# Spreading the 144 w_ada pieces differently: ADA1 16 to 24, ADA2 24/26/30 to 18/18/16

## The chip, the core and the metric

One core of one Trainium2 chip runs the whole program. The metric is device time in microseconds, from a median of repeated runs. The engines that appear below: TensorE (PE; PEld is its weight load), VectorE (DVE), ScalarE (ACT), GpSimd (POOL) and the queue of SyncE (SP), from which nearly all transfers are issued.

## What is computed

Two transformer-like networks run one after the other on 256 tokens of width 1024, in f32. Each has two layers, and a layer is feed-forward, token mixer, feed-forward. In the second network every part is modulated by rows that come from a conditioning vector:

```python
def second_block(x, c, w_ada, b_ada, ...):
    cond = jax.nn.silu(c)
    for l in range(DEPTH):
        mod = cond @ w_ada[l] + b_ada[l]
        sh1, sc1, g1, sh2, sc2, g2, sh3, sc3, g3 = jnp.split(mod[:, None, :], N_MOD, axis=-1)
        y = _swiglu(_modulate(x, sh1, sc1), ffn1_w_gate[l], ffn1_w_up[l], ffn1_w_down[l])
        x = _post_norm(x, y, g1, FFN_RES, ln_gain[l, 0], ln_bias[l, 0])
        y = _token_mixer(_modulate(x, sh2, sc2), w_in[l], w_out[l])
        ...
```

`w_ada` has 2 layers x 1024 x 9216 numbers, 75 MB. It depends on nothing that the program computes, so its product with `cond` can be made at any time before the rows are used.

## The kernel before

**Stages.** The program is twelve parts in a row: block 1 is ffn1, mixer, ffn2 for layer 0 and again for layer 1, block 2 the same. In the trace of before block 2 begins near 1160 us; its parts begin near 1160 (ffn1), 1345 (mixer), 1480 (ffn2), 1680 (ffn1 of layer 1), 1890 (mixer) and 2015 us (ffn2).

**A feed-forward part** (`ffn`) reads its weights in 70 units of at most 512 KB: 48 for gate and up, 22 for down. `unit` takes a raw buffer, loads it from SP's queue, and splits it into a high part (a copy on ACT, `wH`) and a low part (a subtraction on DVE, `wL`); in some units the two parts lie in other buffers, which the trace names `X` or `A`. TensorE multiplies three combinations of the parts. Raw buffers come from a ring, in the order of the code: four named `raw`, and two or four more in cells that the trace names `R` and `S`. Block 1 has eight of them, the last part of block 1 and all of block 2 have six.

**A piece of w_ada** (`ada_pieces`) is 128 rows x 1024 columns, 512 KB. It takes the next raw buffer of the same ring, is loaded from the same queue, and DVE adds it, weighted with `cond`, into the accumulator `aacc`: one instruction for each piece, each needing the one before. Eight pieces make one of the 18 modulation rows. Then `ada_row` splits `aacc` (`aaH` on ACT, `aaL` on DVE), sums over the partitions with two matmuls for each half row into a `tr` bank, adds the bias row (`arow`, on DVE), and writes the half row to memory (`mods`) from SP's queue. `mod_row` reads a finished row back, spread over 128 partitions.

**Where pieces are put.** Units 12 to 69 of a feed-forward part each add a fixed rate to a balance, and each whole number of it calls up a piece:

```python
        if self.local and ADA_FROM <= next(self.count) < ADA_TO:
            self.ada_due += self.ada_rate
        while self.ada_due >= 1:
            self.ada_due -= 1
            next(self.ada_gen, None)
```

The rate is `ADA1 / 62` in block 1 and `ADA2[2 * l + j // 2] / 62` in block 2, so 58 of 62 parts of each constant are made. Where a row is needed and not finished, `mod_row` calls up the missing pieces at once, ahead of whatever the code asks for next:

```python
        while self.mods_done < l * 18 + 2 * q + 2:
            next(self.ada_gen, None)
```

This happens in `rows()`, which a feed-forward part calls after its first eight units and a mixer calls after its input projection.

**What sets the order.** The code above only records operations. `Program.emit` gives each a rank by its longest path to the end, places them on engine timelines with estimated durations, four rounds, and writes the instructions out in the order of the planned starts. Each engine then works its own list in order, SP's queue included.

Of the kernel before, what the change touches and what calls it, by code (L numbers as in the profile page):

```python
# [41 lines left out]
MARGIN_G = 1.0  # L42
HALVES = [slice(0, 512), slice(512, 1024)]
ADA_FROM, ADA_TO = 12, 74
ADA1 = 16
ADA2 = [24, 26, 30, 0]

# [631 lines left out]
class Kern:  # L681
# [1286 lines left out]
    def block1(self):  # L1968
        a = self.a
        with ExitStack() as ctx:  # L1970
# [9 lines left out]
            for (what, l), nxt in zip(steps, pres):  # L1980
                r = {}

                def rows():
                    if not self.sp1:
                        self.setup1()
                        self.ada_rate = ADA1 / (ADA_TO - ADA_FROM)
                    r["post"] = self.rowb(a[what + "_post_g"][l])
# [11 lines left out]

                self.ada_rate = ADA1 / (ADA_TO - ADA_FROM) if what != "mix" and self.sp1 else 0.0  # L2000
                if what == "mix":
# [10 lines left out]
    def block2(self):  # L2012
        a = self.a
        with ExitStack() as ctx:
# [5 lines left out]
            for (what, l, j), nxt in zip(steps, steps[1:] + [None]):  # L2020
# [18 lines left out]
                else:  # L2039
                    self.ada_rate = ADA2[2 * l + j // 2] / (ADA_TO - ADA_FROM)  # L2040
                    self.ffn(a[what + "_w_gate_2"][l], a[what + "_w_up_2"][l], a[what + "_w_down_2"][l], rows, tail, NRL - 2)
# [281 lines left out]
```

## Time and profile before

| | |
|---|---|
| median of 3 runs | 2222.63 us (2222.61 to 2223.07) |
| the profiled execution | 2217.46 us |
| its span, first to last instruction | 2215.7 us |
| TensorE busy / weight load busy | 2150.7 us (97%) / 1911.6 us (86%) |
| VectorE / ScalarE busy | 1613.8 us (73%) / 1019.8 us (46%) |
| read from memory | 451.80 MB, 204 GB/s over the span |

The profiled execution is 1.8 us longer than its span and 5.2 us shorter than the median. TensorE is the busy engine; the 65 us in which it does nothing are made of a start of 8 us, an end of 9 us and many short waits between. The windows view gives for a stretch how long each engine was busy, so length minus busy is its idle time there; the granted clock stands behind POOL's column.

### The profile page before, as it was taken

What the parts mean: (1) busy time and instruction counts of PE and PEld (TensorE: products, weight loads), DVE (VectorE), ACT (ScalarE), POOL (GpSimd) and SP (SyncE); (2) the same over time, 40 slices, a digit from 0 to 9 for tenths busy, and PEclk for the clock granted to TensorE, in tenths of its full rate; (3) what the DMA queues carried; (4) which work ended last, traced back from release to release, by engine and by line L of the source; (5) the groups of instructions that cost most, each with busy time, mean ns of one, the idle gap of its engine ahead of it and who ended that gap; (6) DMA issues with size and microseconds to landing.
All of it is one profiled execution on the core that took longest, in us unless ns stands there. A gap on an engine that the chain in (4) does not pass through costs nothing. (4 is left out here: it accounts for less than half of the span.)

```text
span 2215.7 us, 36384 instructions
## 1 busy us (share of the span) xinstructions
PE 2150.7 (97%) x14604; PEld 1911.6 (86%) x14604; DVE 1613.8 (73%) x2301; ACT 1019.8 (46%) x1440; POOL 47.4 (2%) x73
## 2 busy tenths in 40 slices
PE   8999999999999999999999999999998999999998
PEld 7998988898899798879979988778986987777996
DVE  6666897767666689866667678687878768868554
ACT  6444644545445455454435444534444434544441
POOL 0000001000000000100000000000000000000000
PEclk9999999999999999999999999999999999999999
DMA  9674414767677542466767675468886767537661
GB/s 358 209 246 153 144 57 145 257 213 268 195 242 234 171 135 78 154 220 220 256 212 253 226 266 185 138 206 271 274 281 222 266 224 252 183 126 243 182 194 63
DMA packets 208313, 455.30 MB, mean 205 GB/s; under 512 B 20808, under 2 KB 56008, under 8 KB 208144
## 3 DMA queue, kind: packets, MB, share of 16 engines
q1 hardware_dynamic: 207856, 451.87, 62.5%
q8 instruction: 114, 1.87, 0.3%
q10 hardware_dynamic: 288, 1.11, 0.1%
q14 instruction: 55, 0.45, 0.1%
HBM read 451.80 MB, written 1.12 MB: 204 GB/s over the span
## 5 line engine op out<-in xcount | busy, mean ns | idle before, releaser
L639 DVE TENSOR_TENSOR wL<-raw,wH 128x1024 fp32r<-128x1024 f32 (+1 forms) x375 | 437.8, 1177 | 170.8 <-ACT wH L639 169.2
L639 ACT CAST wH<-raw 128x1024 fp32r<-128x1024 f32 (+1 forms) x375 | 377.4, 1013 | 393.9 <-PE pa L639 118.6
L639 PE MATMUL pa<-hT,wH 128*128 128x256 f32 x3008 | 547.1, 283 | 3.0 <-ACT wH L639 3.0
L639 PEld LDWEIGHTS pa<-hT,wH 128*128 128x128 f32 x3008 | 469.4, 192 | 5.6 <-ACT wH L639 3.4
L639 PE MATMUL pa<-hT,wL 128*128 128x256 f32 x1504 | 425.5, 283 | 0.0
L639 PE MATMUL pa<-hT,X 128*128 128x256 f32 x2400 | 307.9, 283 | 4.0 <-ACT X L639 3.9
L639 PEld LDWEIGHTS pa<-hT,X 128*128 128x128 f32 x2400 | 297.3, 189 | 6.5 <-ACT X L639 4.4
L639 PEld LDWEIGHTS pa<-hT,wL 128*128 128x128 f32 x1504 | 289.1, 192 | 0.2 <-DVE wL L639 0.2
L639 PE MATMUL pj<-wH,hT 128*128 128x256 f32 (+1 forms) x768 | 202.9, 341 | 1.3 <-DVE G L639 0.7
L639 DVE TENSOR_TENSOR X<-raw,X 128x1024 fp32r<-128x1024 f32 (+1 forms) x103 | 117.3, 1139 | 58.9 <-ACT X L639 55.9
L639 DVE TENSOR_TENSOR wL<-R,wH 128x1024 fp32r<-128x1024 f32 (+1 forms) x101 | 119.6, 1185 | 54.9 <-ACT wH L639 54.5
L639 PEld LDWEIGHTS pj<-wH,hT 128*128 128x128 f32 x768 | 132.3, 189 | 24.6 <-issue 5.8
L639 ACT CAST wH<-R 128x1024 fp32r<-128x1024 f32 (+1 forms) x101 | 102.8, 1018 | 105.5 <-PE pa L639 48.8
L639 ACT CAST X<-raw 128x1024 fp32r<-128x1024 f32 (+1 forms) x103 | 101.0, 981 | 79.6 <-PE pa L639 37.7
L639 PE MATMUL pa<-wH,hT 128*128 128x512 f32 x384 | 131.2, 402 | 2.6 <-DVE hT L639 1.1
L639 PE MATMUL pj<-wL,hT 128*128 128x256 f32 (+1 forms) x384 | 126.0, 329 | 3.2 <-DVE wL L639 3.2
L639 PE MATMUL pj<-hT,wH 128*128 128x256 f32 (+1 forms) x672 | 126.8, 288 | 0.1
L639 PEld LDWEIGHTS pj<-hT,wH 128*128 128x128 f32 (+1 forms) x672 | 102.3, 186 | 3.3 <-issue 0.7
L639 DVE SCALAR_TENSOR_TENSOR aacc<-raw,cols,aacc 128x1024 f32<-128x1024 f32 x74 | 94.7, 1280 | 13.8 <-DMA raw<-in_w_ada_dram 13.2
L639 PE MATMUL pb<-wH,A 128*128 128x512 f32 x288 | 102.5, 396 | 0.0
L639 PE MATMUL pa<-wH,A 128*128 128x512 f32 x288 | 102.2, 395 | 0.0
L639 PE MATMUL pj<-hT,wL 128*128 128x256 f32 (+1 forms) x336 | 95.0, 283 | 0.0
(420 smaller groups left out, 3429.6 us busy)
## 6 DMA issues: line engine op xcount, KB each, us to landing
raw<-in_ffn_w_gate_dram SPq DMA_DIRECT2D x110, 512.0 KB
raw<-in_ffn_w_down_dram SPq DMA_DIRECT2D x109, 512.0 KB
raw<-in_w_in_dram SPq DMA_DIRECT2D x108, 512.0 KB
raw<-in_ffn_w_up_dram SPq DMA_DIRECT2D x89, 512.0 KB
raw<-in_w_ada_dram SPq DMA_DIRECT2D x85, 512.0 KB
R<-in_ffn_w_up_dram SPq DMA_DIRECT2D x53, 512.0 KB
R<-in_ffn_w_down_dram SPq DMA_DIRECT2D x53, 512.0 KB
R<-in_w_ada_dram SPq DMA_DIRECT2D x48, 512.0 KB
```

Source lines behind the costliest of these rows:

```text
L639: getattr(self.prog.tc.nc, self.eng).__getattribute__(name)(*[real(x) for x in a], **{q: real(x) for q, x in k.items()})
```

## The change

Two constants change, the sum of the pieces does not.

```diff
-ADA1 = 16
-ADA2 = [24, 26, 30, 0]
+ADA1 = 24
+ADA2 = [18, 18, 16, 0]
```

Counted on SP's list, the parts from the first to the last feed-forward part load these numbers of pieces: before 14, 15, 15, 15 in block 1 and 23, 34, 28, 0 in block 2; now 22, 22, 23, 22 and 17, 17, 15, 4, with 2 more at the end of the last mixer. In the 34 of before there are about 10 that `mod_row` called up at the start of the part, since the rows of layer 1 were due there; now 106 pieces are made by then and 92 are wanted. The last two rows are due at the end of the last mixer and in the last feed-forward part: before, all 144 pieces were made by then, now 138 are, and 6 are called up there.

VectorE at the start of ffn2 of layer 0 in block 2. `hT` is the transposed input of the part for the second half of the tokens, `G` and `A` belong to the part's first products, `x_223` is the second half of the residual. Before:

```order
L639 TENSOR_TENSOR hT_266<-tr,hT_259 128x4x128
L639 SCALAR_TENSOR_TENSOR aacc<-raw,cols,aacc 128x1024 x2
L639 SCALAR_TENSOR_TENSOR aacc<-R,cols,aacc 128x1024 x2
L639 SCALAR_TENSOR_TENSOR aacc<-raw,cols,aacc 128x1024 x2
L639 SCALAR_TENSOR_TENSOR x_223<-x_223,mv,S 128x512 x2
L639 TENSOR_TENSOR G<-G,pa 128x512
L639 TENSOR_TENSOR A<-tr,A 128x4x128
L639 TENSOR_TENSOR aaL<-aacc,aaH 128x512
L639 TENSOR_TENSOR arow<-arow,tr 1x512
L639 TENSOR_TENSOR X<-raw,X 128x1024
```

Now, in the same place:

```order
L639 TENSOR_TENSOR hT_266<-tr,hT_259 128x4x128
L639 SCALAR_TENSOR_TENSOR x_223<-x_223,mv,S 128x512
L639 TENSOR_TENSOR wL<-raw,wH 128x1024
L639 TENSOR_TENSOR wL<-R,wH 128x1024
L639 TENSOR_TENSOR X<-raw,X 128x1024
L639 TENSOR_TENSOR wL<-raw,wH 128x1024 x2
L639 TENSOR_TENSOR X<-R,X 128x1024
L639 TENSOR_TENSOR G<-G,pa 128x512
```

Six pieces in a row and the first half row are gone from there, and the splits of the next units stand directly behind `hT`.

VectorE at the start of ffn2 of layer 1, the last feed-forward part. Before:

```order
L639 TENSOR_TENSOR hT_266<-tr,hT_259 128x4x128
L639 SCALAR_TENSOR_TENSOR x_223<-x_223,mv,L 128x512
L639 TENSOR_TENSOR wL<-raw,wH 128x1024
L639 TENSOR_TENSOR wL<-R,wH 128x1024
L639 TENSOR_TENSOR X<-raw,X 128x1024
L639 TENSOR_TENSOR wL<-raw,wH 128x1024 x2
```

Now:

```order
L639 TENSOR_TENSOR hT_266<-tr,hT_259 128x4x128
L639 SCALAR_TENSOR_TENSOR aacc<-raw,cols,aacc 128x1024 x2
L639 SCALAR_TENSOR_TENSOR aacc<-R,cols,aacc 128x1024 x2
L639 SCALAR_TENSOR_TENSOR x_223<-x_223,mv,L 128x512
L639 TENSOR_TENSOR aaL<-aacc,aaH 128x512
L639 TENSOR_TENSOR X<-raw,X 128x1024
L639 TENSOR_TENSOR wL<-raw,wH 128x1024 x2
```

Four pieces in a row and the first half of the last row came to this place.

SP's queue at the end of the last mixer. Before:

```order
L639 DMA S<-mods 128x1024
L639 DMA raw<-in_w_out_dram 128x1024
L639 DMA R<-in_ffn_w_up_dram 128x2x512
L639 DMA raw<-in_w_out_dram 128x1024
L639 DMA raw<-in_ffn_w_gate_dram 128x2x512
```

Now:

```order
L639 DMA S<-mods 128x1024
L639 DMA raw<-in_w_ada_dram 128x1024
L639 DMA R<-in_ffn_w_up_dram 128x2x512
L639 DMA raw<-in_w_ada_dram 128x1024
L639 DMA raw<-in_w_out_dram 128x1024
L639 DMA mods<-arow 1x512
L639 DMA R<-in_ffn_w_up_dram 128x2x512
L639 DMA S<-mods 128x1024
L639 DMA raw<-in_w_out_dram 128x1024
```

The last unit of `w_out` now stands behind two pieces, behind the write of a half row and behind the read of that row. On VectorE's list two pieces, two instructions on the half row and two 128x1024 products with the late row stand there in front of the mixer's tail; none of them stood there before.

## Rows read from the trace of the kernel before

**Rows 1.** The page: busy time of the engines, share of the span, instructions.

```profile
PE 2150.7 (97%) x14604; PEld 1911.6 (86%) x14604; DVE 1613.8 (73%) x2301; ACT 1019.8 (46%) x1440; POOL 47.4 (2%) x73
```

**Rows 2.** Windows: stretch, length, busy time by engine, granted clock, DMA share, GB/s.

```profile
640.00:720.00 80.00, 80.00 (x629) 77.55 (x628) 53.94 (x59) 39.11 (x49) 0.00 (x0) 1.00 0.72 232
1200.00:1320.00 120.00, 120.00 (x852) 112.13 (x851) 86.14 (x93) 54.05 (x66) 0.00 (x0) 1.00 0.74 242
1352.00:1362.00 10.00, 7.58 (x47) 6.14 (x47) 9.49 (x18) 1.86 (x4) 0.92 (x1) 1.00 0.54 166
1488.00:1516.00 28.00, 22.92 (x127) 18.89 (x126) 24.08 (x26) 8.33 (x11) 0.00 (x0) 0.96 0.80 261
1510.00:1520.00 10.00, 7.70 (x49) 7.50 (x50) 5.50 (x6) 6.01 (x7) 0.00 (x0) 0.83 0.89 297
1520.00:1640.00 120.00, 120.00 (x891) 113.98 (x890) 95.01 (x103) 55.11 (x69) 0.00 (x0) 1.00 0.82 274
1655.00:1670.00 15.00, 13.41 (x57) 10.16 (x56) 10.80 (x12) 5.04 (x5) 0.00 (x0) 1.00 0.59 186
1675.00:1700.00 25.00, 20.07 (x89) 14.77 (x90) 22.95 (x31) 9.45 (x12) 0.92 (x1) 1.00 0.79 259
1812.00:1822.00 10.00, 6.50 (x34) 5.68 (x34) 5.60 (x7) 4.50 (x6) 0.00 (x0) 0.83 0.54 198
1885.00:1903.00 18.00, 13.59 (x73) 9.91 (x72) 17.25 (x27) 4.22 (x6) 0.99 (x1) 1.00 0.81 245
1990.00:2012.00 22.00, 21.52 (x99) 16.61 (x98) 19.03 (x31) 9.05 (x13) 0.93 (x1) 1.00 0.57 194
2020.00:2030.00 10.00, 6.86 (x33) 4.97 (x32) 9.31 (x15) 1.17 (x2) 0.93 (x1) 1.00 0.82 263
2030.00:2058.00 28.00, 28.00 (x194) 25.87 (x193) 24.23 (x27) 16.09 (x18) 0.00 (x0) 1.00 0.80 249
```

**Rows 3.** Groups by shape, VectorE: one piece, and the addition of one half row.

```profile
L639 DVE SCALAR_TENSOR_TENSOR aacc<-raw,cols,aacc 128x1024 f32<-128x1024 f32 x74 | 94.7, 1280 | 13.8 <-DMA raw<-in_w_ada_dram 13.2
L639 DVE TENSOR_TENSOR arow<-arow,tr 1x512 f32<-1x512 f32 x36 | 24.1, 670 | 12.0 <-PE tr L639 11.6 <-DMA arow<-in_b_ada_dram 0.4
L639 DVE TENSOR_SCALAR arow<-arow 1x512 f32<-1x512 f32 x24 | 9.8, 410 | 0.2
```

**Rows 4.** Timeline of the start of ffn2, layer 0: VectorE, SP's queue, TensorE.

```profile
1488.53 2.59 DVE L639 SCALAR_TENSOR_TENSOR aacc<-raw,cols,aacc 128x1024 f32<-128x1024 f32 x2
...
1495.12 1.70 SPq L639 DMA_DIRECT2D raw<-in_ffn_w_gate_dram  x2
...
1512.26 1.21 PE L639 MATMUL pa<-hT,wH 128*128 128x256 f32 x8 [3.03 <-ACT wH L639]
```

**Rows 5.** Timeline of the end of that part: VectorE, SP's queue, ScalarE.

```profile
1657.60 1.28 DVE L639 SCALAR_TENSOR_TENSOR aacc<-R,cols,aacc 128x1024 f32<-128x1024 f32 x1
...
1658.90 0.34 SPq L639 DMA_DIRECT2D R<-in_ffn_w_down_dram  x1
...
1663.38 1.04 ACT L639 CAST A<-R 128x1024 fp32r<-128x1024 f32 x1 [5.63 <-DMA R<-in_ffn_w_down_dram]
```

**Rows 6.** TensorE's timeline and SP's waits (us, times, longest), 1812 to 1822.

```profile
1817.30 3.02 PE L639 MATMUL pa<-hT,X 128*128 128x256 f32 x11 [3.40 <-ACT X L639]
...
SPq L639 <- DVE X L639: 6.0, 1, 6.0
```

**Rows 7.** Timeline of VectorE in two turns between parts of block 2.

```profile
1675.79 1.28 DVE L639 SCALAR_TENSOR_TENSOR aacc<-raw,cols,aacc 128x1024 f32<-128x1024 f32 x1
...
1886.63 0.67 DVE L639 TENSOR_TENSOR arow<-arow,tr 1x512 f32<-1x512 f32 x1
```

**Rows 8.** Timeline of the last mixer's end: SP's queue, ScalarE, TensorE.

```profile
1992.56 0.33 SPq L639 DMA_DIRECT2D raw<-in_w_out_dram  x1
...
1998.22 1.05 ACT L639 CAST wH<-raw 128x1024 fp32r<-128x1024 f32 x1 [1.76 <-DMA raw<-in_w_out_dram]
...
2011.67 1.04 PE L639 MATMUL tr<-con,h 128*128 128x128 f32 x8
```

## Prediction

> **What bounds the kernel now.** The page comes first: TensorE is busy for 97% of the span [rows 1], so nothing that is added beside it costs time unless TensorE comes to wait. The next view is therefore the windows, read for what TensorE lacks in each stretch. Inside the feed-forward parts it lacks nothing: 80.00 of 80 us in a part of block 1 that carries 15 pieces, 120.00 of 120 in ffn1 of block 2 with 23, and 120.00 of 120 even in the gate and up products of the part with 34 [rows 2]. What is lacking lies at certain places of block 2, and the third view, the timelines, says what is done there. At the start of ffn2 of layer 0, VectorE works six pieces one after the other; the raw buffers are in their hands, the next gate loads leave SP's queue only at 1495.12, and TensorE ends up waiting 3.03 us for a weight [rows 4]. So the price of a piece is not its 1.28 us on VectorE [rows 3] but the time at which it gives its raw buffer back, and whose load stands behind it.
>
> **What the move takes away in block 2.** Five places, each by length minus TensorE's busy time, compared with a like place that has no pieces in its way [rows 2].
> - Start of ffn2, layer 0: 28 - 22.92 = 5.1 us idle between 1488 and 1516. The same stretch of the last feed-forward part, which has no pieces, has 28.00 of 28. Behind it the granted clock is 0.83 over the ten microseconds from 1510, which is a time at the lower level of 1.2 GHz instead of 2.4 and costs 1.7 us more. Together 6.8. In the new order the row of VectorE there is the one that the last part had before, so I take all of it as saved.
> - End of that part: 15 - 13.41 = 1.6. A piece held `R` until 1658.9, and the load of a down unit that waited for it came 4.5 us later [rows 5].
> - Turn from there to ffn1 of layer 1: 25 - 20.07 = 4.9, against 10 - 6.86 = 3.1 in the turn to the last part: 1.8 above the like. Pieces stand between the tail and the transposed input [rows 7]; in the new order none does.
> - Last gate and up units of ffn1, layer 1, near 1814: 10 - 6.50 = 3.5, and the clock 0.83 again for 1.7: 5.2. SP stood 6.0 us behind one buffer there [rows 6].
> - Turn from there to the last mixer: 18 - 13.59 = 4.4 against 10 - 7.58 = 2.4 in the other mixer of block 2: 2.0. A half row's additions stand among the splits and the transposes there [rows 7]; in the new order they are gone.
>
> That is 6.8 + 1.6 + 1.8 + 5.2 + 2.0 = 17.4 us in all. The first, third and fifth hang on instructions whose place I can see emptied: 10.6, taken in full. The second and fourth, 6.8, hang on which buffer of the ring stood behind which, and with 17 pieces instead of 34 and 15 instead of 28 the ring still turns. ffn1 of layer 0 with 23 pieces had neither, so the bounds are 0 and 6.8, and I take half, 3.4. Saved: 14.0 us.
>
> **What the move adds in block 1.** Seven or eight pieces more in each of four parts: 8 x 1.28 = 10.2 us of VectorE and 4.2 MB a part. VectorE was busy 53.94 of 80 us there and has some 26 us free in each 80; the transfers were at 0.72 of their time [rows 2]. The nearest row is the part with 23 pieces, which has the new number, only six raw buffers where block 1 mostly has eight, and no idle time inside. I take nothing; the upper bound is the stall near 1814 once in each of the four parts, 4 x 5.2 = 20.8. If a part does not hide them, each piece that TensorE waits for costs up to 1.28 us. The turns between the parts of block 1 keep one piece here and lose one there; I take nothing for them either.
>
> **What it adds at the end of block 2.** Six pieces are called up late, where before none was.
> - End of the last mixer. VectorE's list gets two pieces (2.56), the half row (0.67 + 0.41) [rows 3] and two products with the late row (128x1024 as a piece is, so by its row 2.56) in front of the tail: 6.2 us. In the 22 us there VectorE was idle for 22 - 19.03 = 3.0 [rows 2]. What doesn't fit is 3.2. The transfers give the same size: the last `w_out` load was issued at 1992.56 and reached ScalarE at 1998.22 [rows 8]; now it stands behind the write of a half row and the read of that row, about four microseconds later. TensorE was not waiting before its transposes at 2011.67 [rows 8], so most of a delay shows. I take 3.0, with bounds of 0 and 6.2.
> - Start of the last part. Four pieces in a row instead of six, and no second batch behind them as ffn2 of layer 0 had; the next gate loads stand ahead of the pieces on SP's queue or just behind. Bounds 0 and 6.8 (the whole loss of that other start). I take 0.5, near the lower end, because the first eight units are in hand and give TensorE some 10 us of products (48 for half the tokens, at 6.86 us for 33 in the turn [rows 2]) over four pieces' 5.1.
>
> One rule of the skill speaks against this. In the trace the clock fell behind the single waits of 3.03 and 3.40 us [rows 4, 6], and stayed at 1.00 through 4.9 us of idle time in several short waits between 1675 and 1700 [rows 2]. The Trainium skill (TensorE: Matmul & The Clock Gate, section "A second HAM failure mode: psum-queue depth-cycling") says that frequent very short idle times between groups of matmuls can make the clock swing too. By that rule the short waits at the new place would cost another 1.7 us, and the forecast would be 2213.8; by the row they cost no clock. I go by the row.
>
> **The sum.** -14.0 + 3.0 + 0.5 = -10.5 us. On the profiled execution, 2217.46, that gives 2207.0. The median of the runs lies 5.2 us above that execution, and I take the difference as it is: 2222.63 - 10.5 = 2212.1, told as 2212.
>
> **The rivals.**
> - *The waits belong to the order, not to the number of pieces.* The planner writes the whole program in another order, and a ring whose buffers change hands with any piece can stall at new places. For: the stall near 1814 came in a part with fewer pieces than its neighbour, which had none at that point. Against: the stretches of the parts with 15 and 23 pieces show none [rows 2]. Two new stalls of that kind anywhere, 2 x 5.2, give 2222.5: no change.
> - *The late pieces cost what the early ones did.* The last mixer's end takes all of its 6.2 and the start of the last part all of its 6.8: -14.0 + 13.0 = -1.0, so 2221.6. For: the same code at the same kind of place lost 6.8. Against: four pieces, not ten, and two of the six are in the mixer.
> - *Block 1 pays (slower).* One mechanism: at the end of the gate and up products the last units are small, a piece's buffer holds SP's queue up, and TensorE waits as it did near 1814, once in each part of block 1. At 5.2 each it decides from the third stall on, since two cost 10.4 and the forecast saves 10.5. With all four: 2212.1 + 20.8 = 2232.9. For: 22 pieces are nearer to 28 than 15 were. Against: eight buffers, and the part with 23.
> - *All is saved.* The second and fourth place go in full and the late pieces hide: 2222.63 - 17.4 = 2205.2.
> - *That the change does not do what it says* can be left aside: the counts on the new list are 22, 22, 23, 22, 17, 17, 15 and 6 late.
>
> **How the numbers follow.** Forecast 0.47; all is saved 0.12; waits by order 0.17; late pieces 0.14; block 1 pays 0.10. What a measurement of this kernel tells from no change is about 0.2%, 4.4 us: faster is below 2218.2, slower above 2227.1. Faster: the forecast, all saved, and two thirds of the late pieces' case, whose cost spreads from the 3.5 I took to 13.0: 0.68. Same: the rest of that case and the waits by order: 0.22. Slower: 0.10. The range runs from all saved, 2205, to 2224, a little above the two cases of no change; block 1's case and a sliver on either side are left out.
>
> **What would show it.** Right: windows of the new kernel with TensorE full through the first 30 us of ffn2 of layer 0, the turns to ffn1 and to the mixer of layer 1 with about 3.1 and 2.4 us idle, two drops of the clock fewer in block 2, and some 3 us of new idle time around the last mixer's end, most of it before its transposes. The feed-forward parts of block 1 stay without idle time inside. Wrong: waits of 3 us or more with a load of w_up or w_down as their cause in block 1; a clock below 1.00 in the last part; or idle time of TensorE that is gone from the five places while the total of it is not smaller.

## The result, and the profile after

| | before | after |
|---|---|---|
| median | 2222.62 us (2214.18 to 2223.07) | 2193.71 us (2192.09 to 2195.12) |
| the profiled execution | 2217.46 us | 2192.09 us |
| its span | 2215.7 us | 2190.3 us |
| TensorE busy | 2150.7 us | 2142.4 us |

The ratio is 0.988, with a 95% interval from 0.987 to 0.990: 1.2% faster. The median fell by 28.9 us and the profiled execution by 25.4, where 10.5 was forecast. The time lies below the range. The kernel before was timed beside every experiment below; the median of all its 39 runs is 2219.4 us, 25.7 above the changed kernel's, so the 25.4 of the profiles is the better size.

The page of the changed kernel, its line that answers to [rows 1]:

```profile
PE 2142.4 (98%) x14604; PEld 1909.5 (87%) x14604; DVE 1614.9 (74%) x2301; ACT 1021.6 (47%) x1440; POOL 48.4 (2%) x73
```

Time in which TensorE does nothing fell from 65.0 to 47.9 us. The windows of the changed kernel, each laid as far behind its part's first transposes as its counterpart in [rows 2], or as far ahead of the next part's where it shows the end of a part: block 1, the turn to the first mixer, the start and the end of ffn2 of layer 0, the turn to ffn1 of layer 1, that part's last gate and up units, the turn to the last mixer, that mixer's end, and two of the last part's start.

```profile
640.00:720.00 80.00, 80.00 (x640) 78.09 (x639) 54.42 (x61) 36.47 (x46) 0.00 (x0) 1.00 0.71 225
1354.00:1364.00 10.00, 9.32 (x59) 7.97 (x58) 8.89 (x16) 3.89 (x6) 0.92 (x1) 1.00 0.27 88
1488.00:1516.00 28.00, 28.00 (x195) 26.05 (x194) 25.60 (x27) 15.05 (x17) 0.00 (x0) 1.00 0.88 289
1642.00:1657.00 15.00, 15.00 (x66) 12.19 (x66) 8.57 (x11) 4.43 (x5) 0.00 (x0) 1.00 0.89 310
1662.00:1687.00 25.00, 24.76 (x116) 20.05 (x115) 22.75 (x31) 8.76 (x12) 0.92 (x1) 1.00 0.62 195
1799.00:1809.00 10.00, 10.00 (x45) 8.07 (x44) 8.11 (x9) 5.57 (x6) 0.00 (x0) 1.00 0.86 273
1856.00:1874.00 18.00, 17.32 (x95) 14.32 (x94) 16.55 (x26) 4.05 (x7) 0.99 (x1) 1.00 0.42 147
1962.00:1984.00 22.00, 18.63 (x80) 13.77 (x81) 17.13 (x24) 8.56 (x11) 0.93 (x1) 1.00 0.67 231
1992.00:2002.00 10.00, 6.80 (x29) 4.53 (x27) 9.48 (x15) 1.64 (x3) 0.93 (x1) 1.00 0.86 290
2002.00:2030.00 28.00, 27.31 (x180) 24.76 (x181) 25.71 (x29) 16.64 (x21) 0.00 (x0) 1.00 0.86 284
```

Block 1 has nothing idle inside in its window, as before. All five places are mended, and the turns beyond what was held possible: the turn to ffn1 of layer 1 lacks 0.24 us where 3.1 was to be left, the turn to the last mixer 0.68 where 2.4 was, and the turn to the first mixer, which the sum did not contain, 0.68 instead of 2.42. The new loss is at the last mixer's end: 3.4 us instead of 0.5. SP's queue with its longest wait from 1962 to 1967 us, ScalarE and TensorE there:

```profile
1961.72 0.28 SPq L639 DMA_DIRECT2D mods<-arow  x1
...
1966.35 0.33 SPq L639 DMA_DIRECT2D S<-mods  x1
SPq L639 <- DMA mods<-arow: 3.1, 1, 3.1
1966.79 0.37 SPq L639 DMA_DIRECT2D raw<-in_w_out_dram  x1
...
1971.70 1.04 ACT L639 CAST wH<-raw 128x1024 fp32r<-128x1024 f32 x1 [3.91 <-DMA raw<-in_w_out_dram]
...
1972.79 0.74 PE L639 MATMUL pg<-wH,X 128*128 128x512 f32 x2 [2.25 <-ACT wH L639]
```

The write of the late half row leaves for memory at 1961.72, and SP stands 3.1 us until that write has landed and the row can be read back at 1966.35. The last `w_out` load stands behind the read and leaves at 1966.79, and TensorE waits 2.25 us in the middle of that product. The two late pieces are added only from 1968.97 on, when that load has left, so what holds it back is the row's way through memory and not the buffers of those two.

The table that is used from here on has the length of each part of block 2 and of the last feed-forward part of block 1, from its first transposes to those of the next part (the last to the last matmul), in us. It is worked out from the timelines; behind the length stands the number of pieces that are loaded in that part. All of these feed-forward parts have six raw buffers.

| kernel | block 1, last | ffn1 l0 | mixer l0 | ffn2 l0 | ffn1 l1 | mixer l1 | ffn2 l1 |
|---|---|---|---|---|---|---|---|
| before | 190.6 (15) | 195.1 (23) | 127.4 | 205.3 (34) | 208.0 (28) | 128.4 | 194.5 (0) |
| after | 191.9 (22) | 192.8 (17) | 125.2 | 192.3 (17) | 192.0 (15) | 129.6 (2) | 197.3 (4) |
| e1_no_bunch | 191.0 (18) | 193.8 (22) | 127.0 | 192.7 (22) | 210.8 (29) | 128.4 | 194.0 (0) |
| e2_even34 | 191.5 (21) | 192.9 (15) | 125.2 | 201.4 (33) | 198.4 (14) | 125.2 | 194.0 (0) |
| e3_no_late | 192.0 (22) | 193.3 (19) | 125.1 | 199.3 (19) | 196.5 (17) | 125.2 | 196.4 (0) |
| e5_early | 190.6 (15) | 193.7 (23) | 125.1 | 207.3 (34) | 196.3 (28) | 127.2 | 196.8 (0) |
| e6_nolate_early | 192.7 (23) | 193.2 (19) | 125.2 | 192.3 (19) | 192.7 (17) | 125.2 | 194.5 (0) |
| e7_thin | 190.6 (15) | 193.8 (23) | 126.9 | 203.4 (34) | 202.5 (28) | 129.8 | 194.5 (0) |
| e9_b1_alone | 191.9 (22) | 196.7 (23) | 128.7 | 197.0 (24) | 193.3 (8) | 125.2 | 194.0 (0) |
| e10_near | 191.9 (23) | 193.7 (17) | 125.2 | 193.1 (17) | 192.5 (17) | 125.9 | 194.5 (0) |

From before to after, 33.6 us went in four neighbouring parts of block 2, 29.0 of them in ffn2 of layer 0 and ffn1 of layer 1, and 8.2 came back, in block 1 and the last two parts.

### The profile page after: what moved, and what is told of

Read it like the earlier page. It is cut to its first block, busy times and chain, and to the rows that moved or that the text cites. A ratio compares the mean times of both kernels' runs of the same rounds, so it can differ in the third digit from the quotient of the medians.

```text
span 2190.3 us, 36375 instructions
## 1 busy us (share of the span) xinstructions
PE 2142.4 (98%) x14604; PEld 1909.5 (87%) x14604; DVE 1614.9 (74%) x2301; ACT 1021.6 (47%) x1440; POOL 48.4 (2%) x73
## 5 line engine op out<-in xcount | busy, mean ns | idle before, releaser
L639 DVE TENSOR_TENSOR wL<-raw,wH 128x1024 fp32r<-128x1024 f32 (+1 forms) x362 | 422.9, 1179 | 160.9 <-ACT wH L639 158.8
L639 ACT CAST wH<-raw 128x1024 fp32r<-128x1024 f32 (+1 forms) x362 | 363.9, 1015 | 375.3 <-PE pa L639 133.9
L639 DVE TENSOR_TENSOR wL<-R,wH 128x1024 fp32r<-128x1024 f32 (+1 forms) x111 | 129.9, 1174 | 40.7 <-ACT wH L639 39.3
L639 ACT CAST wH<-R 128x1024 fp32r<-128x1024 f32 (+1 forms) x111 | 111.5, 1008 | 86.4 <-PE pa L639 44.1
L639 DVE SCALAR_TENSOR_TENSOR aacc<-raw,cols,aacc 128x1024 f32<-128x1024 f32 x78 | 99.8, 1279 | 12.4 <-DMA raw<-in_w_ada_dram 12.0
```

The source lines that it names most:

```text
L639: getattr(self.prog.tc.nc, self.eng).__getattribute__(name)(*[real(x) for x in a], **{q: real(x) for q, x in k.items()})
```

## The experiments

The theory of the prediction is that a piece costs where its raw buffer is given back late. Three readings of it were to be told apart: that the number of pieces in a part sets its loss, that the ten called up in a row do, or that the loss lies where a piece stands near the turn to the next part; against all three stands that a new order puts its stalls anywhere. Where a diff of constants has no `-` lines, its `+` lines replace the constants of the kernel before.

### Numbers of pieces: bunch, even load, no late pieces

**e1_no_bunch**

```diff
-ADA1 = 16
-ADA2 = [24, 26, 30, 0]
+ADA1 = 19
+ADA2 = [24, 24, 30, 0]
```

> Pieces per feed-forward part 17, 18, 18, 18 and 22, 22, 29, 0, one of them called up. Against the kernel before, the bunch of ten at the start of ffn2 of layer 0 is gone and that part falls from 34 to 22; ffn1 of layer 1 keeps its load (29 for 28). Number of pieces: ffn2 of layer 0 falls from 205.3 to about 194 us, ffn1 of layer 1 stays at about 208; total near 2211. Bunch alone: only the start of ffn2 of layer 0 is mended, 6.8 us, and its end and the next turn keep their waits; near 2216. Order by chance: losses of the same kind at other places, and ffn1 of layer 1 may come out anywhere from 192 to 208.

Measured: 2208.9 us, 0.995 (0.993 to 0.997). ffn2 of layer 0 is 192.7 long, as in the changed kernel, though it has 22 pieces and not 17. The start of the part, in the window that answers to the fourth of [rows 2]:

```profile
1488.00:1516.00 28.00, 28.00 (x196) 26.10 (x195) 24.80 (x26) 15.17 (x18) 0.00 (x0) 1.00 0.88 285
```

ffn1 of layer 1 kept its loss (210.8). Number and place both fit; if the bunch alone were the cause, part of the loss would have stayed in ffn2.

**e2_even34**

```diff
+ADA1 = 22
+ADA2 = [16, 36, 16, 0]
```

> Pieces 20, 21, 20, 21 and 15, 33, 14, 0, none called up, none late. ffn2 of layer 0 has nearly as many as before (33 for 34), but evenly spread, and ffn1 of layer 1 has as few as in the changed kernel. Number of pieces: ffn2 of layer 0 keeps most of its loss, some 8 to 13 us over the 192.3 of the changed kernel; total about 2199 to 2204. Bunch: the part takes about 194 (half rows alone make it 2 us longer), total about 2191. Order by chance: the part anywhere from 193 to 206.

Measured: 2202.4 us, 0.992 (0.990 to 0.994). 33 pieces without a bunch still cost 9.1 us in their part against the changed kernel's 17 (1.9 of it four half rows), so the bunch is not the whole of it. And ffn1 behind it, with 14 pieces, takes 198.4 instead of 192.0. Its turn is where that is lost, as the window of 25 us around it shows:

```profile
1668.00:1693.00 25.00, 18.87 (x76) 13.34 (x75) 23.01 (x32) 7.33 (x11) 1.53 (x2) 0.93 0.73 237
```

SP's queue says whose loss it is (its longest wait between 1659 and 1670 us, and the transfer that follows it):

```profile
SPq L639 <- DVE arow L639: 9.4, 1, 9.4
1669.21 0.25 SPq L639 DMA_DIRECT2D mods<-arow  x1
```

The write of a half row, made from pieces of the part ahead, stood in the queue for 9.4 us until VectorE had finished it, with the gate loads of ffn1 behind it; the next of them left at 1671.20. The loss of a part with few pieces was left by the pieces of the part ahead of it.

**e3_no_late**

```diff
+ADA1 = 24
+ADA2 = [20, 20, 20, 0]
```

> Pieces 22, 22, 23, 22 and 19, 19, 17, 0: the changed kernel without the six late ones. Late pieces cost what the profile of the changed kernel shows at the last mixer's end and the last part's start (1.2 + 2.8 us more than before): total about 2190, the last mixer 128 and the last part 194.5 long. Number of pieces: two or three more in three parts, still below the 22 or 23 that cost 2 us; at most 1 us given back. Order by chance: within 4 us of 2193.7 on either side, the last mixer as long as before or not.

Measured: 2197.6 us, 0.990 (0.988 to 0.992), where 2190 was expected. The last mixer went to 125.2, so the late pieces cost what was thought and more, but ffn2 of layer 0, with 19 pieces, took 199.3. Number alone can't give that, since 22 took 192.7. The turn behind it shows the mechanism (SP's queue, VectorE, ScalarE, TensorE; a row of a queue runs from its first to its last transfer's issue):

```profile
1651.31 5.73 SPq L639 DMA_DIRECT2D raw<-in_ffn_w_gate_dram  x3
...
1655.36 1.28 DVE L639 SCALAR_TENSOR_TENSOR aacc<-raw,cols,aacc 128x1024 f32<-128x1024 f32 x1
...
1661.39 2.00 ACT L639 CAST wH<-raw 128x1024 fp32r<-128x1024 f32 x2 [5.78 <-DMA raw<-in_ffn_w_gate_dram]
1662.47 1.23 DVE L639 TENSOR_TENSOR wL<-raw,wH 128x1024 fp32r<-128x1024 f32 x1 [3.50 <-ACT wH L639]
1663.61 1.28 DVE L639 TENSOR_TENSOR h<-pb,L 128x512 f32<-128x512 f32 x2
...
1669.89 1.12 PE L639 MATMUL tr<-con,h 128*128 128x128 f32 x4 [5.35 <-DVE h L639]
```

A piece is added at 1655.36 and ends at 1656.64; the third of the gate loads can leave only then, since 1651.31 + 5.73 is 1657.04. SP's own waits there are 0.7 us for that piece and, just before it, 2.3 for VectorE's split of a down unit, so one piece is the last link of the delay and not all of it. The load lands for ScalarE at 1661.39. The low part of that unit, which TensorE won't want for ten microseconds (its first product of the next part starts at 1676.94), stands on VectorE's list ahead of the tail `h<-pb` and waits 3.50 us for it. The tail starts late, and TensorE waits 5.35 us for the transposes. Here the price of a piece is paid by what stands behind the late load on VectorE's list.

### Place of the pieces: away from the turn

**e5_early**: the pieces of each part are spread over units 12 to 59 instead of 12 to 69, the last (the code says 74, but a part has 70 units); the numbers stay, but for one piece that moves within block 1.

```diff
-ADA_FROM, ADA_TO = 12, 74
-ADA1 = 16
-ADA2 = [24, 26, 30, 0]
+ADA_FROM, ADA_TO = 12, 60
+ADA1 = 14.8
+ADA2 = [23, 24, 28, 0]
```

> The kernel before with the same number of pieces in every part (14, 15, 15, 15, 23, 34, 28, 0, ten of them called up), but from units 12 to 59 instead of 12 to 73: none in the last ten units, so none near the turn to the next part. Turn: the losses at the turns go, 6 us in the turn to ffn1 of layer 1, 3 in that to the last mixer, 2 in that to the first mixer of block 2; the bunch at the start of ffn2 of layer 0 stays with its 9; total about 2210. Number: the parts stay at 205 and 208 long, total about 2220. Order by chance: one of the three turns is mended and another place gets a new loss; total 2210 to 2225.

Measured: 2207.3 us, 0.994 (0.992 to 0.996). With 28 pieces ffn1 of layer 1 takes 196.3 instead of 208.0, and the mixer behind the part with 23 takes 125.1 instead of 127.4. ffn2 of layer 0, whose pieces are called up at its start, keeps its loss (207.3). So number is refuted as the whole cause, and place holds. Two things did not come as expected: the wait near 1814, which is not at a turn, went too, and the last mixer gained 1.3 and not 3: its turn still lacks 2.2 us.

**e6_nolate_early**: the same window for the numbers of e3.

```diff
+ADA_FROM, ADA_TO = 12, 60
+ADA1 = 22.3
+ADA2 = [19, 19, 17, 0]
```

> The kernel without late pieces (22, 22, 22, 23, 19, 19, 17, 0), again from units 12 to 59 only. Turn: the 5.35 us wait before the transposes at the end of ffn2 of layer 0, which came from a split held up behind pieces' buffers in front of the tail, goes with its two drops of the clock; that part falls from 199.3 to about 192.5, ffn1 of layer 1 from 196.5 to about 193; total about 2187. Number: as with the pieces to unit 73, about 2197. Order by chance: anywhere from 2187 to 2200, with a loss at another place than the end of ffn2 of layer 0.

Measured: 2186.8 us, 0.985 (0.983 to 0.986): as the theory of the turn had it, and below the changed kernel, whose interval (0.987 to 0.990) does not reach it. The turn to ffn1 of layer 1, the turn to the last mixer, and that mixer's end:

```profile
1662.00:1687.00 25.00, 24.32 (x114) 19.84 (x114) 23.15 (x31) 10.36 (x14) 1.00 (x2) 1.00 0.63 204
1855.00:1873.00 18.00, 17.32 (x98) 14.68 (x97) 16.59 (x28) 2.72 (x5) 0.99 (x1) 1.00 0.43 135
1962.00:1984.00 22.00, 21.28 (x99) 16.31 (x98) 18.80 (x28) 11.07 (x16) 0.93 (x1) 1.00 0.57 196
```

Against the changed kernel it gains 4.4 us in the last mixer and 2.8 in the last part; together 7.2 is the price of the six late pieces, 0.9 of it two half rows.

**e10_near**: a neighbour, with pieces to unit 69 again.

```diff
+ADA1 = 25
+ADA2 = [18, 18, 18, 0]
```

> A neighbour of the kernel without late pieces: 23, 23, 24, 23 and 17, 17, 17, 0, from units 12 to 73 again. Number alone: below 2193, since no part of block 2 has more than 17. Turn: whether a piece's buffer stands behind the split that is ahead of the tail depends on the order, so each turn may lose 0 or 3 to 7 us; total 2186 to 2200, and a loss, if there is one, stands at a turn. Order anywhere: a loss of 3 us or more inside a part, away from the turns.

Measured: 2192.2 us, 0.988 (0.986 to 0.990). No feed-forward part of block 2 is longer than 194.5, and no turn behind one has a wait over 0.9 us. Number alone would give this too; it fell with e3 and e5. With 17 to 19 pieces up to the end of a part the turn may be hit (e3) or not (e10, after); in e6, with the same 19 kept away from it, it was not.

### What a piece costs: its time or its buffer

**e7_thin**: the kernel before, in its order; seven of eight pieces add one column only, so the modulation rows are left incomplete. `thin` replaces the operands where the instruction is written, after the planner has placed the full one.

```diff
-                        self.stt(acc, rv, cc, acc, ALU.mult, ALU.add)
+                        self.stt(acc, rv, cc, acc, ALU.mult, ALU.add,
+                                 thin=(acc[:, :1], rv[:, :1], cc, acc[:, :1], ALU.mult, ALU.add))
```

> The kernel before, word for word the same order on every engine, but seven of eight pieces add only one column of 1024 (the rest of the rows is left out); loads, buffers and queue places are as before. VectorE loses some 125 x 1.2 = 150 us of work. If a piece costs by its time on VectorE: the three turns and the bunch lose their waits, total 2195 to 2200. If it costs by the buffer and the queue place alone: the loads come as late as before, the total falls by the bunch's four or five us at most, about 2215. If both: ffn2 of layer 0 improves at its start and the turn to ffn1 of layer 1 does not, about 2207.

Measured: 2212.5 us, 0.996 (0.994 to 0.997). One of the piece's groups (of duration the least, the median and the most, in ns), and windows of four of the five places: the start of ffn2 of layer 0, the turn behind it, the place of the wait near 1814, and the turn to the last mixer:

```profile
L639 DVE SCALAR_TENSOR_TENSOR aacc<-raw,cols,aacc x74: 201/215/222, 67.4 to 1858.1; 128x1 f32<-128x1 f32 x74
```

```profile
1486.00:1514.00 28.00, 22.97 (x127) 19.32 (x126) 14.64 (x26) 8.66 (x12) 0.00 (x0) 0.94 0.77 262
1670.00:1695.00 25.00, 18.80 (x85) 13.74 (x84) 20.68 (x30) 8.65 (x11) 1.51 (x2) 1.00 0.74 243
1810.00:1820.00 10.00, 10.00 (x53) 8.38 (x51) 5.73 (x9) 4.49 (x5) 0.00 (x0) 1.00 0.84 293
1880.00:1898.00 18.00, 14.36 (x66) 11.86 (x67) 15.71 (x25) 5.02 (x8) 0.99 (x1) 0.81 0.68 216
```

126 x (1280 - 215) ns = 134 us of VectorE's work are gone, and the kernel gains 7.5 us. TensorE still lacks 5.0 us at the start, 6.2 at the turn to ffn1 and 3.6, with a drop of the clock, at the turn to the last mixer. At these three VectorE's time is not the price; the buffer, the queue place and the load behind them are. At the other two it is part of it: the wait near 1814 went, where SP stood behind VectorE [rows 6], and so did the small ones at the end of ffn2.

Which loads stand behind is on SP's queue. The turns to ffn1 and to the last mixer, with SP's longest wait there and, for the first, the load that follows it, of before (1662 to 1680 and 1870 to 1890 us) and then of e7 (1662 to 1676 and 1862 to 1880):

```profile
SPq L639 <- DVE aacc L639: 11.4, 2, 10.6
1677.10 0.37 SPq L639 DMA_DIRECT2D raw<-in_ffn_w_gate_dram  x1
...
SPq L639 <- DVE arow L639: 9.2, 1, 9.2
```

```profile
SPq L639 <- DVE aacc L639: 10.8, 2, 10.0
1672.32 0.37 SPq L639 DMA_DIRECT2D raw<-in_ffn_w_gate_dram  x1
...
SPq L639 <- DVE arow L639: 9.7, 1, 9.7
```

A piece (at the first turn) or a half row's write (at the second) stands on VectorE's list within the part's tail or behind it. It keeps SP for some ten microseconds, and the next part's loads stand behind it however short the addition is. In both kernels only 4 units of the next part had been issued before the transposes at each of these turns; in the changed kernel it was 9 and 8, in e6 8 and 8, at the turn that e2 lost 4, and at the one where e5 still lacks 2.2 us 4. e3 lost its turn in the other way, on VectorE's list, with 8 issued.

### Block 1: does the ring of eight hide the pieces?

**e4_heavy1**

```diff
+ADA1 = 36
+ADA2 = [6, 6, 0, 0]
```

> Pieces 33, 34, 34, 33 in block 1 and 6, 4, 0, 0 in block 2, none called up. Number of pieces, whatever the ring: each part of block 1 loses what ffn2 of layer 0 lost with 34, 10 to 13 us, and the total is 2225 to 2240. Number against the size of the ring: block 1 has eight raw buffers, its parts stay within 3 us of 192 (four more half rows at 0.47 us each), and the total is about 2189 to 2195. Order by chance: some of the four parts lose 3 us or more and others, with the same count, nothing.

Measured: 2210.6 us, 0.996 (0.995 to 0.997), neither expectation's time. The four parts of block 1 became 3.3, 4.7, 6.1 and 12.6 us longer than before. The half rows that they got more (below) are about 2 us in each. The first three have eight raw buffers, the fourth six; the fourth loses 10 us, as the part with 34 pieces of block 2 did. The mixer behind the third lost 6.1.

**e8_heavy6**: the same with six buffers in all.

```diff
-                             NRL if nxt is not None else NRL - 2)
+                             NRL - 2)
```

> The kernel with 33, 34, 34, 33 pieces in block 1, with six raw buffers instead of eight in the first three feed-forward parts too (the fourth has six in both). Size of the ring: those three parts, which took 195.0, 197.0 and 198.4 us with eight, become as long as the fourth, about 203; total about 2210.6 + 19 = 2229. Number whatever the ring: they stay within 2 us of where they were, total about 2211. Order by chance: one of them gains 5 us or more, another loses.

Measured: 2244.5 us, 1.010 (1.008 to 1.012). The first three parts grew by a further 9.8, 10.1 and 7.7 us, to 204.8, 207.1 and 206.1, and the mixers behind the first and the third by 4.5 and 5.6. The fourth part, whose buffers did not change, became 2.9 shorter, so a difference of that size can be the order's. And some 6 of the first part's 9.8 us are lost before its first piece (the start that e12 shows below).

**e12_after6**: the changed kernel with the edit of e8.

> The changed kernel with six raw buffers instead of eight in the first three feed-forward parts of block 1 too (22, 22, 23 pieces there; the fourth part had 22 with six in both). The prediction took block 1's extra pieces at nothing because a part with 23 pieces and six buffers had no idle time inside. If that is the reason, six buffers do no harm at 22 and 23 pieces: the three parts stay within 1.5 us of 192.4, 193.2 and 192.8, total 2192 to 2198. If block 1's two more buffers are what hid the pieces: each of the three parts loses 3 to 6 us, total 2203 to 2212. Order by chance: one part loses 5 us at its turn, the others nothing.

Measured: 2218.1 us, 0.999 (0.998 to 1.000): with two buffers fewer in three parts of block 1 the whole gain is gone. The parts with 22, 22 and 23 pieces take 204.9, 193.2 and 197.5 instead of 192.4, 193.2 and 192.8. Two windows of the first part, its start and its turn:

```profile
18.00:38.00 20.00, 15.80 (x59) 11.82 (x58) 9.31 (x12) 8.17 (x13) 0.56 (x1) 0.83 0.86 305
205.00:220.00 15.00, 9.51 (x37) 7.58 (x36) 8.15 (x13) 7.21 (x16) 1.42 (x3) 0.77 0.31 91
```

and the chain of its turn, on VectorE, ScalarE and TensorE:

```profile
198.08 1.27 DVE L639 SCALAR_TENSOR_TENSOR aacc<-raw,cols,aacc 128x1024 f32<-128x1024 f32 x1
...
203.16 1.05 ACT L639 CAST wH<-raw 128x1024 fp32r<-128x1024 f32 x1 [5.90 <-DMA raw<-in_w_in_dram]
...
208.24 1.99 ACT L639 CAST wH<-raw 128x1024 fp32r<-128x1024 f32 x2 [2.73 <-DMA raw<-in_w_in_dram]
...
213.32 1.11 PE L639 MATMUL tr<-con,h 128*128 128x128 f32 x4 [5.49 <-DVE h L639]
```

It is the chain of e3, with ScalarE's copies of the next part's weights ahead of the tail, which ScalarE can go on with only at 210.14. The wait in the first window, at the program's start, comes before the first piece, which VectorE adds at 49.5; it is the smaller ring's and not theirs. It takes about 7 of the 24 us: 4.2 idle, where the changed kernel has 0.3 in the same window at a clock of 1.00, and 3.4 by the clock. Some 15 stand at the turns of block 1. No run has six buffers in the first three parts with 15 pieces there, so how much of those 15 the smaller ring would cost without the extra pieces is not shown. What is on record is the fourth part, which has six in every run: 190.6 us with 15 pieces, 191.9 with 22, 203.1 with 33.

### One part of the change alone, and the half rows

**e9_b1_alone**

```diff
-ADA1 = 16
+ADA1 = 24
```

> Only the first half of the change: ADA1 is 24, the numbers of block 2 stay at 24, 26, 30. Pieces 22, 22, 23, 22 and 23, 24, 8, 0; they run out in ffn1 of layer 1, and none is called up or late. If fewer pieces called up and fewer near the later turns are what the change gained: ffn1 of layer 0 and the mixer behind it stay at 195 and 127.4, ffn2 of layer 0 falls to 193 to 196, ffn1 of layer 1 to about 191, the last part stays at 194.5; total about 2195. If block 1's heavier load costs by itself: its feed-forward parts grow by more than their half rows (3.6 us together), and the total stays above 2200. Order by chance: a turn with 23 or 24 pieces ahead of it loses 5 us, as one with 19 did; total 2195 to 2205.

Measured: 2200.6 us, 0.991 (0.990 to 0.993). The first constant alone gains 18 us; with it no piece is called up, and they run out in ffn1 of layer 1. Losses stay at the turns around the parts with 23 and 24 pieces (196.7 and 197.0, the mixer between them 128.7), which the time expected left out; and the second mixer of block 1, which has no pieces, took 3.0 us more, nearly all of it a stretch at half clock (0.86 over the 25 us from 900, 3.5 us lost).

**e11_thin_rows**: e6 in its order, with 64 of 512 columns in the sums of each half row, so that the rest of the rows is left out.

```diff
-        self.mm(ps[0:1], self.onesr, H, True, False)
-        self.mm(ps[0:1], self.onesr, L, False, True)
+        self.mm(ps[0:1], self.onesr, H, True, False, thin=(ps[0:1, :64], self.onesr, H[:, :64]))
+        self.mm(ps[0:1], self.onesr, L, False, True, thin=(ps[0:1, :64], self.onesr, L[:, :64]))
```

> The kernel with pieces from units 12 to 59 and none late, word for word the same order, but the two sums over the partitions of each half row take 64 of 512 columns (the rest of the rows is left out): 72 matmuls, each of which took 0.23 us from its start to the next. If they are TensorE time on the path: about 0.17 us less for each, total about 2186.8 - 12 = 2175, and each feed-forward part shorter by 0.35 us for every half row in it. If they lie in time that TensorE has to spare: no change, 2186 to 2188.

Measured: 2179.2 us, 0.982 (0.981 to 0.984): 7.6 us less than e6, not 12. In the parts whose waits are those of e6 the gain is 0.31 to 0.32 us a half row (1.89 for six, 1.56 and 1.60 for five, 1.25 for four), near the 0.35 expected; the last part of block 1 lost more at its turn (its wait before the transposes is 2.21 us and not 1.21), and the program's first part, with four, gained only 0.6. A half row is TensorE time on the path, about 0.47 us from its first matmul's start to the next product's.

## Why the prediction was wrong, point by point

The side and the mechanism were right; the size was less than half. By the steps:

- **Start of ffn2, layer 0** (6.8 taken in full): right. 28.00 of 28, and the clock there at 1.00.
- **End of that part and the stall near 1814** (6.8, of which half was taken): both went in full. That is 3.4 missed.
- **The two turns** (1.8 and 2.0): they gave 4.9 - 0.24 = 4.7 and 4.4 - 0.68 = 3.7. This is the step that failed. A place was priced against a "like" place, and the like places were the wrong ones: the turn to the last part follows a mixer, while this one follows a feed-forward part, and the other mixer's turn had 23 pieces ahead of it. What a turn costs without pieces near it is in e6: 0.68 and 0.68. 4.6 missed. The instructions pointed at were the right ones: SP stood 10.6 us for the piece at 1675.79 and 9.2 for the write of a half row just ahead of the one in [rows 7]. So the mechanism held, and the term was too small, 3.8 for a measured 8.4.
- **The part with 23 pieces taken as free**: inside it was, but its turn was not. ffn1 of layer 0 and the mixer behind it, not in the sum at all, became 4.5 us shorter, 0.9 of it two half rows. e5 shows it with the number kept: 125.1 for that mixer.
- **Idle time as the price**: the record of a 512-column matmul is 0.40 us long while the next starts 0.23 us behind it, so each wait behind such a matmul reads about 0.16 short. Two rows of TensorE in the changed kernel, one behind the other, show it:

```profile
1655.88 0.40 PE L639 MATMUL pa<-wH,B 128*128 128x512 f32 x1
1656.12 0.40 PE L639 MATMUL pa<-wL,B 128*128 128x512 f32 x1
```

In ffn2 of layer 0 and ffn1 of layer 1 the idle time fell by 15.9 us, the time between starts beyond the usual 0.12 and 0.23, without what the clock took, by about 20: some 4 us that the windows do not show.
- **Block 1** (0 taken): no waits came, so right, but not for the reason given. The part with 23 pieces and six buffers was taken as proof that six suffice; e12 lost 24 us with six, some 15 of it at turns. So with six the term would have been wrong, though not in every part: e12's second, with 22 pieces, kept its 193.2. And the parts did grow, by 0.4 to 1.4 us, together 3.4, for eight more half rows; the prediction counted a half row's additions on VectorE and not its two matmuls. Since the 36 half rows only move, that is given back in block 2.

The PE column of the windows of the half rows' tile, for the last feed-forward part of block 1 and ffn2 of layer 0, before and after (each `x` is one of the two matmuls):

```profile
957.00:1147.00 190.00, 1.19 (x3) 0.25 (x3) 2.75 (x4) 2.47 (x4) 1.00 0.72 237
1470.00:1675.00 205.00, 3.64 (x9) 0.74 (x9) 5.46 (x8) 4.93 (x8) 0.99 0.79 264
```

```profile
960.00:1152.00 192.00, 2.46 (x6) 0.50 (x6) 4.11 (x6) 3.71 (x6) 0.99 0.76 248
1470.00:1662.00 192.00, 1.59 (x4) 0.34 (x4) 2.76 (x4) 2.49 (x4) 1.00 0.76 250
```

- **The late pieces** (3.0 + 0.5): 7.2 by e6. The idle time at the mixer's end was right in size (3.4 less 0.5 is 2.9), and of the two reasons given it was the second, the load behind the half row's write and read. But 2.25 of it lies in the product with `w_out` and only 0.8 before the transposes. The last part's start was put too low, at 0.5 where 2.8 came, and the half rows were missing.
- **The median** was taken as 5.2 us above the profiled execution. After, the two are 1.6 apart, and by all its runs before was 1.9 above. That makes some 3.6 us of the miss, and none of it is the change's.

The profiled execution fell 14.9 us further than forecast. The steps add 3.4 (second and fourth place), 4.6 (turns), 4.5 (ffn1 of layer 0 and its mixer), some 4 (waits read short) and 3.8 (eight half rows fewer in ffn2 of layer 0 and ffn1 of layer 1), and take away 4.2 (block 1 with its mixers) and 3.7 (late pieces). That makes about 12; where the rest went is open.

Of the rivals, "all is saved" was nearest. "Block 1 pays" did not come about, but e8 and e12 show that block 1 does pay with six buffers: at the program's start and at the turns, not at the end of the gate and up products where the rival had it. "The late pieces cost what the early ones did" was half right. That waits belong to the order holds in a narrower form than was put: at 17 to 24 pieces in six buffers some turns are hit and some are not. Why the wait near 1814 went in e5, where the numbers stayed, is open.

## What to carry to other kernels

A side stream that shares a ring of buffers with the main one costs where a load is late and something urgent stands behind it on an in-order engine: look at the turns, where early splits of the next part are listed ahead of the tail, and keep the side stream away from them. Read the transfer queue there, and count the loads of the next part that leave before the turn. Price a loss against the same kind of place without the suspect in it, and look first whether the place taken as like carries the suspect itself. Where waits are short, read the starts of matmuls, not the gaps between their records.

## What the runs showed of the hardware

The clock did not follow the waits alone. Windows of 10 us around and behind the 1.7 and 1.8 us waits before the transposes of two block 1 parts, of before and then of after:

```profile
384.00:394.00 10.00, 8.25 (x31) 6.23 (x31) 9.71 (x13) 7.04 (x11) 0.56 (x1) 0.83 0.71 220
955.00:965.00 10.00, 8.12 (x38) 6.07 (x38) 9.66 (x13) 6.42 (x11) 0.56 (x1) 1.00 0.66 219
```

```profile
386.00:396.00 10.00, 8.31 (x38) 6.23 (x39) 9.72 (x14) 7.35 (x12) 0.56 (x1) 1.00 0.71 226
958.00:968.00 10.00, 8.12 (x32) 6.27 (x32) 9.65 (x13) 7.03 (x11) 0.56 (x1) 0.83 0.69 216
```

The same wait was followed by the lower level (1.2 GHz) in one execution and not in the other, at either place. And the turn to the last part, with 2.7 us idle in short waits, stood at 1.00 before [rows 2] and after, but e3 and e5 have there, in this order:

```profile
2003.00:2018.00 15.00, 12.32 (x44) 9.45 (x44) 11.00 (x15) 5.35 (x7) 0.93 (x1) 0.77 0.65 211
```

```profile
2009.00:2024.00 15.00, 12.33 (x44) 9.56 (x44) 10.97 (x16) 5.44 (x7) 0.93 (x1) 0.77 0.57 179
```

In each of them 3.4 us are lost. The prediction read the row of one execution as "short waits cost no clock". In after that held; in e3 and e5 it did not. That agrees with the rule of the Trainium skill that was weighed against it (TensorE: Matmul & The Clock Gate, section "A second HAM failure mode: psum-queue depth-cycling"). In the windows shown a drop cost 1.7 us of work (0.83 over 10 us) or 3.4 (0.77 over 15).
